# Two-PSUM-bank multiplies and transposed key sums in a strided-attention kernel

## The chip, the cores and the metric

The kernel runs on one core of one Trainium2 chip. The metric is device time in microseconds (us), the median of several executions. The time before is 129.94 us (three runs, 129.86 to 130.21). A profile covers one execution; its span is about 2 us shorter than the device time, because the span runs from the first instruction to the last. Fast runs are the undisturbed ones, slow runs the others.

Engines in the profile: PE (TensorE matmul), PEld (its weight loads), DVE (VectorE), ACT (ScalarE), POOL (GpSimd), SP (which issues the transfers). PSUM is the memory that the matmuls write into. In this kernel a one-bank PSUM tile holds 512 float32 values in each of the 128 partitions, a two-bank tile 1024. "Tail" below means the time from the end of VectorE's last multiply to the end of the span.

## The reference

```python
Q, K, V: (8, 12, 1024, 64) float32, stride 64
k = K[:, :, ::64]; v = V[:, :, ::64]              # 16 keys per head
scores = q @ k.T / 8
w = exp(scores - max); w = w / (sum(w) + 1e-10)
result = w @ v                                     # same shape as V
```

Each of the 96 heads has 1024 queries and only 16 keys. There is little arithmetic: 25 MB of queries come in, 25 MB of results go out.

## The kernel before

Four heads make a group, so there are 24 groups, and a group is one 1 MB load and one 1 MB store. GpSimd casts the queries to bf16, VectorE transposes them in 32x32 blocks, PE makes scores, ScalarE takes the exponential, PE makes key sums and outputs, and VectorE multiplies the outputs by the reciprocal sums. These are the parts that the change touches:

```python
psum_o = ... bufs=4        # one bank each;  OBUFS = 9 output tiles

def keys(m):               # m = 0 at the start, 1 and 2 after groups 2 and 4
    for h in range(4):
        nc.vector.tensor_scalar(out=k_m[...h], in0=kr, scalar1=slot_m[:, h:h+1], ..., op0=mult)
    for u in range(2):
        kp = psum_o.tile([P, 2, 2, 2, 4 * NK], FP32)     # one bank
        ... four matmuls into kp ...
        nc.scalar.copy(k_t half, kp)

def sums(g):
    sm = psum_s.tile([P, 2, 8, 2], FP32)
    for i in range(8):
        nc.tensor.matmul(sm[:, :, i], lhsT=wt[g][:, i], rhs=s_sel, ...)   # 4 columns
    nc.vector.reciprocal(rec[g], sm ...)

def outputs(g, c):         # c = 0..3
    ps = psum_o.tile([P, 2, 2, 2 * D], FP32)             # one bank
    for i in range(2):
        nc.tensor.matmul(ps[:, :, i], lhsT=wt[g][:, 2 * c + i], rhs=vb[g], ...)
    nc.vector.tensor_tensor(out=out_sb[g][...], in0=ps, in1=rec[g] broadcast, op=mult)   # 512

for g in range(NG):
    transpose(g + 2); sums(g); outputs(g, 0); outputs(g, 1); scores(g + 1)
    outputs(g, 2); outputs(g, 3); values(g + 2); cast(g + 3)
    if g in (2, 4): keys(g // 2)
    store(g); load(g + QBUFS)
# ... cut: set-up, scores, values, cast, load, store ...
```

The softmax here doesn't subtract the row's maximum and nothing guards it: scores larger than these inputs give would overflow.

Of the kernel before, what the change touches and what calls it, by code (L numbers as in the profile page):

```python
# [11 lines left out]
FP32 = mybir.dt.float32  # L12
BF16 = mybir.dt.bfloat16
# [6 lines left out]
def _ap_with(ap: bass.AP, new_ap, extra_offset: int = 0) -> bass.AP:  # L20
    return dataclasses.replace(
        ap, ap=[list(p) for p in new_ap], offset=ap.offset + extra_offset
    )
# [22 lines left out]



@with_exitstack
def kernel(  # L50
    ctx: ExitStack,
# [7 lines left out]
    nc = tc.nc  # L59

    B, H, S, D = Q.shape
    NK = S // stride
    scale = 1.0 / math.sqrt(D)

    P = 128
# [4 lines left out]
    KW = P + NK  # L70
    assert B * H == NG * HG and S == 1024 and D == 64 and NK == 16
    QBUFS = 10
    OBUFS = 9

    const = ctx.enter_context(tc.tile_pool(name="const", bufs=1))
    qn_pool = ctx.enter_context(tc.tile_pool(name="qn", bufs=QBUFS))
    out_pool = ctx.enter_context(tc.tile_pool(name="outsb", bufs=OBUFS))
    qb_pool = ctx.enter_context(tc.tile_pool(name="qb", bufs=2))
    qt_pool = ctx.enter_context(tc.tile_pool(name="qt", bufs=2))
    vb_pool = ctx.enter_context(tc.tile_pool(name="vb", bufs=3))  # L80
    rec_pool = ctx.enter_context(tc.tile_pool(name="rec", bufs=2))
    psum_sc = ctx.enter_context(tc.tile_pool(name="psc", bufs=2, space=bass.MemoryType.PSUM))
    psum_o = ctx.enter_context(tc.tile_pool(name="po", bufs=4, space=bass.MemoryType.PSUM))
    psum_s = ctx.enter_context(tc.tile_pool(name="psm", bufs=2, space=bass.MemoryType.PSUM))

    ctx.enter_context(tc.manual_schedule())
# [7 lines left out]
    def load(g):  # L94
        qn[g] = qn_pool.tile([P, 32 * D], FP32, name="qn", tag="qn")
        n = P if g < 2 else 32
        _copy(nc, qn[g], _ap_with(Q, [[HG * SD // n, n], [1, HG * SD // n]], g * HG * SD))
# [12 lines left out]
    perm_k = const.tile([P, 2, 2, 2, NK], BF16, name="perm_k")  # L110
# [10 lines left out]
    for c in range(2):  # L121
        for a in range(2):
            for e in range(2):
                nc.gpsimd.tensor_copy(
                    out=perm_v[:, c, a, :, e], in_=id_v[:, c, :, a]
                )

    k_t = const.tile([P, NG, 2, KW], BF16, name="k_t")
    nc.vector.memset(k_t[:, 0:8], 0.0)  # L129
    w_bufs = []  # L130
    for i in range(3):
# [7 lines left out]
        out=slot_i, in0=iota_p, scalar1=4, scalar2=3,  # L139
# [4 lines left out]
    s_sel = const.tile([P, 4], BF16, name="s_sel")  # L144
    nc.vector.tensor_scalar(  # L145
        out=s_sel, in0=col4, scalar1=slot_f, scalar2=None, op0=ALU.is_equal
    )
    slot_m = const.tile([P, 4], FP32, name="slot_m")
    nc.vector.tensor_copy(out=slot_m, in_=s_sel)
    mask = const.tile([P, 4, D], BF16, name="mask")  # L150
# [2 lines left out]
    k_m = const.tile([P, NC, 2, 4, 32], BF16, name="k_m")  # L153
# [4 lines left out]
    def keys(m):  # L158
        kr = k_raw[:, 4 * m : 4 * m + 4].rearrange("p n (q f) -> p n f q", f=2)
        for h in range(4):  # L160
            nc.vector.tensor_scalar(  # L161
                out=k_m[:, 4 * m : 4 * m + 4, :, h], in0=kr,
                scalar1=slot_m[:, h : h + 1], scalar2=None, op0=ALU.mult,
            )
        for u in range(2):
            kp = psum_o.tile([P, 2, 2, 2, 4 * NK], FP32, name="kp", tag="o")
            for i in range(2):
                for f in range(2):
                    nc.tensor.matmul(  # L169
                        kp[:, i, :, f],  # L170
                        lhsT=k_m[:, 4 * m + 2 * u + i, f].rearrange("p h q -> p (h q)"),
                        rhs=perm_k.rearrange("p c a b k -> p c (a b k)"),
                        start=True, stop=True,
                    )
            g0 = 8 * m + 4 * u
            dst = k_t[:, g0 : g0 + 4]
            nc.scalar.copy(  # L177
                _ap_with(dst, [dst.ap[0], [KW, 8], [32, 4], [1, NK]], extra_offset=NK),
                kp.rearrange("p i c f (s k) -> p (i c f) s k", s=4),
            )  # L180


    def value_rows():
# [10 lines left out]
    qb, qt, wt, vb, rec, out_sb = {}, {}, {}, {}, {}, {}  # L194


    def values(g):
        vb[g] = vb_pool.tile([P, 4, D], BF16, name="vb", tag="vb")
        nc.gpsimd.tensor_tensor(  # L199
            out=vb[g], in0=mask,  # L200
            in1=v_rep[:, g // 2, g % 2].unsqueeze(1).to_broadcast([P, 4, D]),
            op=ALU.mult,
        )

    def cast(g):
        qb[g] = qb_pool.tile([P, 32 * D], BF16, name="qb", tag="qb")
        nc.gpsimd.tensor_copy(out=qb[g], in_=qn[g])  # L207

    def transpose(g):
        qt[g] = qt_pool.tile([P, 32 * D], BF16, name="qt", tag="qt")  # L210
        nc.vector.transpose(qt[g].bitcast(I32), qb[g].bitcast(I32))  # L211

    def scores(g):
        sc = psum_sc.tile([P, 512], FP32, name="sc", tag="sc")
        q = qt[g]
        for e in range(2):
            for f in range(2):
                nc.tensor.matmul(  # L218
                    sc, lhsT=k_t[:, g, f, NK * (1 - e) : NK * (1 - e) + P],
                    rhs=_ap_with(  # L220
                        q, [q.ap[0], [2 * D, 8], [16 * D, 2], [2, 32]],
                        extra_offset=D * e + f,
                    ),
                    start=e + f == 0, stop=e + f == 2,
                )
        w = wt[g] = w_bufs[g % 3]
        for a in range(2):
            wa = w[64 * a : 64 * a + 64]
            nc.scalar.activation(  # L229
                out=_ap_with(wa, [wa.ap[0], [P, 8], [1, 2], [2, 32]], extra_offset=64 * a),  # L230
                in_=sc[64 * a : 64 * a + 64].rearrange("p (t x q) -> p t x q", t=8, x=2),
                func=AF.Exp, bias=0.0, scale=scale,
            )

    def sums(g):
        sm = psum_s.tile([P, 2, 8, 2], FP32, name="sm", tag="sm")
        for i in range(8):
            nc.tensor.matmul(  # L238
                sm[:, :, i], lhsT=wt[g][:, i], rhs=s_sel, start=True, stop=True
            )  # L240
        rec[g] = rec_pool.tile([P, 2, 16], FP32, name="rec", tag="rec")
        nc.vector.reciprocal(rec[g], sm.rearrange("p b i e -> p b (i e)"))  # L242

    def outputs(g, c):
        if c == 0:
            out_sb[g] = out_pool.tile([P, 2, 16, D], FP32, name="out_sb", tag="out_sb")
        ps = psum_o.tile([P, 2, 2, 2 * D], FP32, name="o_ps", tag="o")
        for i in range(2):
            nc.tensor.matmul(  # L249
                ps[:, :, i], lhsT=wt[g][:, 2 * c + i],  # L250
                rhs=vb[g].rearrange("p s d -> p (s d)"),
                start=True, stop=True,
            )
        nc.vector.tensor_tensor(  # L254
            out=out_sb[g][:, :, 4 * c : 4 * c + 4],
            in0=ps.rearrange("p b i (e d) -> p b (i e) d", e=2),
            in1=rec[g][:, :, 4 * c : 4 * c + 4].unsqueeze(3).to_broadcast([P, 2, 4, D]),
            op=ALU.mult,
        )

    def store(g):
        o = out_sb[g]
        _copy(
            nc,
            _ap_with(out, [[16 * D, P], [2 * SD, 2], [1, 16 * D]], g * HG * SD),
            _ap_with(o, [o.ap[0], [1, 1], [1, 32 * D]]),
        )

    keys(0)
    cast(0)  # L270
    transpose(0)
    scores(0)
    value_rows()
    values(0)
# [4 lines left out]
    for g in range(NG):  # L279
        if g + 2 < NG:  # L280
            transpose(g + 2)
        sums(g)
        outputs(g, 0)
        outputs(g, 1)
        if g + 1 < NG:
            scores(g + 1)
        outputs(g, 2)
        outputs(g, 3)
        if g + 2 < NG:
            values(g + 2)  # L290
        if g + 3 < NG:
            cast(g + 3)
        if g in (2, 4):
            keys(g // 2)
        store(g)
        if g + QBUFS < NG:
            load(g + QBUFS)
# [35 lines left out]
```

## Time and profile before

| before | value | where it is read |
|---|---|---|
| span | 127.7 us | page, first line |
| DMA queue, share of 16 engines | 96.8%, 51.12 MB | page, part 3 |
| VectorE busy | 109.2 us, 85% | page, part 1 |
| VectorE's cycle per group | 3.97 us | timeline of VectorE |
| end of the last multiply | 119.97 us | timeline of VectorE |
| from there to the end of the span | 7.7 us | difference |

The page says that two resources are nearly full. These are its parts 1, 3 and 4 (engines, the DMA queue with its share, and the chain of work that ended last), and two groups of its part 5, whose columns are busy us and mean ns of one, then idle time in front and its releaser:

```profile
PE 73.3 (57%) x508; PEld 38.6 (30%) x508; DVE 109.2 (85%) x170; ACT 39.6 (31%) x55; POOL 66.7 (52%) x69
...
q1 hardware_dynamic: 7904, 51.12, 96.8%
...
DVE 2%; DVEq 0%; issue 0%
...
L254 DVE TENSOR_TENSOR out_sb<-o_ps,rec 128x512 f32<-128x512 f32 x96 | 59.9, 685 | 4.8 <-PE o_ps L249 2.6
...
L242 DVE RECIPROCAL rec<-sm 128x32 f32<-128x32 f32 x24 | 7.8, 326 | 0.3 <-PE sm L238 0.3
```

The chain covers only 2% of the span: it is followed from the last multiply back to 117.14 us and breaks off there. Such a short chain is no proof of a limit (the run with the large memset below shows the same 2%, with VectorE late). The sign of a DMA limit is the queue, which is nearly full to the end. But VectorE is hardly slower. This is its timeline of the kernel before (start, duration, instruction):

```profile
62.61 1.24 DVE L211 STREAM_TRANSPOSE qt<-qb 128x1024 int32<-128x1024 int32 x1
63.77 0.32 DVE L242 RECIPROCAL rec<-sm 128x32 f32<-128x32 f32 x1
64.18 2.48 DVE L254 TENSOR_TENSOR out_sb<-o_ps,rec 128x512 f32<-128x512 f32 x4
66.58 1.24 DVE L211 STREAM_TRANSPOSE qt<-qb 128x1024 int32<-128x1024 int32 x1
```

From one query transpose to the next is 3.97 us with no gap. Read the distances between starts, not the durations: independent instructions overlap by about 0.08 us, and an instruction that needs the result of the last starts a little after its end (here 0.09 us: the reciprocal ends at 64.09, the first multiply starts at 64.18).

### The profile page before, as it was taken

The numbers are of one execution on the slowest core, as the hardware profiler recorded it, in microseconds if no ns is written. First come the engines' busy times: TensorE is split into PE (matmuls) and PEld (weight loads), VectorE is DVE, ScalarE is ACT, GpSimd is POOL, SyncE is SP. The second block draws the span as 40 slices with busy tenths as digits, with TensorE's granted clock in tenths as the row PEclk, the third lists the DMA queues.
The fourth block names the chain that finished last, engine by engine and source line by source line (L and its number), as shares of the span: only waits on it lengthen the run. The fifth ranks groups of instructions, "written<-read, shape, count | busy, mean of one in ns | idle before, by whom it ended". The sixth has DMA issues, their size and how long they took to land. (4 is left out here: it accounts for less than half of the span.)

```text
span 127.7 us, 1518 instructions
## 1 busy us (share of the span) xinstructions
PE 73.3 (57%) x508; PEld 38.6 (30%) x508; DVE 109.2 (85%) x170; ACT 39.6 (31%) x55; POOL 66.7 (52%) x69
## 2 busy tenths in 40 slices
PE   0006767974476097866675579755567776674000
PEld 0003233441433063333342234432234323342000
DVE  6997468999979987899999999999999999999500
ACT  3003404224244134344424440444431344323000
POOL 8980499675217605387767635787555727000000
PEclk9999999999779855599999965799998559999555
DMA  2999989898998998989989999999999999999981
GB/s 70 380 322 459 482 339 482 349 482 359 462 472 336 503 400 377 505 346 431 493 344 439 454 385 436 441 408 452 426 398 464 385 421 431 426 416 428 421 372 46
DMA packets 7913, 51.23 MB, mean 401 GB/s; under 512 B 3872, under 2 KB 3872, under 8 KB 3872
## 3 DMA queue, kind: packets, MB, share of 16 engines
q1 hardware_dynamic: 7904, 51.12, 96.8%
q8 instruction: 4, 0.07, 0.2%
q14 instruction: 5, 0.04, 0.1%
HBM read 25.95 MB, written 25.17 MB: 400 GB/s over the span
## 5 line engine op out<-in xcount | busy, mean ns | idle before, releaser
L254 DVE TENSOR_TENSOR out_sb<-o_ps,rec 128x512 f32<-128x512 f32 x96 | 59.9, 685 | 4.8 <-PE o_ps L249 2.6
L229 ACT ACTIVATE w<-sc 64x512 bf16<-64x512 f32 x48 | 35.1, 732 | 60.0 <-PE sc L218 56.7
L207 POOL CAST qb<-qn 128x2048 bf16<-128x2048 f32 x24 | 45.5, 1898 | 0.4 <-DMA qn<-in_Q_dram 0.4
L249 PE MATMUL o_ps<-vb,w 128*128 128x256 bf16 x192 | 38.0, 321 | 2.4 <-DVE out_sb L254 1.4
L199 POOL TENSOR_TENSOR vb<-mask,v_rep 128x256 bf16<-128x256 bf16 x24 | 16.1, 670 | 40.3 <-PE o_ps L249 35.4
L218 PE MATMUL sc<-qt,k_t 128*128 128x512 bf16 x96 | 32.7, 472 | 1.5 <-DVE qt L211 1.2
L211 DVE STREAM_TRANSPOSE qt<-qb 128x1024 int32<-128x1024 int32 x24 | 29.7, 1237 | 1.6 <-POOL qb L207 1.6
L249 PEld LDWEIGHTS <-w 128*128 128x128 bf16 x192 | 19.3, 110 | 16.2 <-issue 8.6
L238 PE MATMUL sm<-s_sel,w 128*128 128x4 bf16 x192 | 8.7, 167 | 22.1 <-ACT w L229 22.1
L238 PEld LDWEIGHTS <-w 128*128 128x128 bf16 x192 | 6.9, 100 | 30.1 <-ACT w L229 29.6
L218 PEld LDWEIGHTS <-k_t 128*128 128x128 bf16 x96 | 10.8, 114 | 12.0 <-issue 6.5
L169 PE MATMUL kp<-perm_k,k_m 128*128 128x128 bf16 x24 | 3.1, 311 | 17.5 <-DVE k_m L161 17.5
L242 DVE RECIPROCAL rec<-sm 128x32 f32<-128x32 f32 x24 | 7.8, 326 | 0.3 <-PE sm L238 0.3
L169 PEld LDWEIGHTS <-k_m 128*128 128x128 bf16 x24 | 2.3, 141 | 18.2 <-DVE k_m L161 18.2
L177 ACT CAST k_t<-kp 128x512 bf16<-128x512 f32 x6 | 3.2, 590 | 14.1 <-PE kp L169 14.1
L161 DVE TENSOR_SCALAR k_m<-k_raw,slot_m 128x256 bf16<-128x256 f32 x12 | 6.8, 626 | 0.0
L192 DVE CAST v_rep<-vp 128x384 bf16<-128x384 f32 x4 | 2.2, 558 | 2.6 <-PE vp L188 2.6
L135 POOL MEMSET k_t<- 128x4608 bf16 x1 | 3.9, 3938 | 0.0
L145 DVE TENSOR_SCALAR s_sel<-col,slot_f 128x4 bf16<-128x4 int16 x1 | 3.2, 3155 | 0.1
L188 PE MATMUL vp<-v_bf,perm_v 128*128 128x384 bf16 x4 | 2.0, 489 | 0.8 <-DVE v_rep L192 0.6
L177 ACT ACT_TABLE_LOAD x1 | 1.3, 1283 | 2.1 <-DVE k_t L129 2.1
L129 DVE MEMSET k_t<- 128x1152 uint32 x1 | 1.0, 1018 | 1.0 <-PEq L314 1.0
(17 smaller groups left out, 6.3 us busy)
## 6 DMA issues: line engine op xcount, KB each, us to landing
qn<-in_Q_dram SPq DMA_DIRECT2D x24, 1024.0 KB, 13.9
out_dram<-out_sb SPq DMA_DIRECT2D x24, 1024.0 KB, 12.0
k_raw<-in_K_dram SPq DMA_DIRECT2D x1, 384.0 KB, 4.1
v_raw<-in_V_dram SPq DMA_DIRECT2D x1, 384.0 KB, 7.2
```

Source lines behind the costliest of these rows:

```text
L161: nc.vector.tensor_scalar(out=k_m[:, 4 * m : 4 * m + 4, :, h], in0=kr, scalar1=slot_m[:, h : h + 1], scalar2=None, op0=ALU.mult,)
L169: nc.tensor.matmul(kp[:, i, :, f], lhsT=k_m[:, 4 * m + 2 * u + i, f].rearrange("p h q -> p (h q)"), rhs=perm_k.rearrange("p c a b k -> p c ...
L177: nc.scalar.copy(_ap_with(dst, [dst.ap[0], [KW, 8], [32, 4], [1, NK]], extra_offset=NK), kp.rearrange("p i c f (s k) -> p (i c f) s k", s=4),)
L199: nc.gpsimd.tensor_tensor(out=vb[g], in0=mask, in1=v_rep[:, g // 2, g % 2].unsqueeze(1).to_broadcast([P, 4, D]), op=ALU.mult,)
L207: nc.gpsimd.tensor_copy(out=qb[g], in_=qn[g])
L211: nc.vector.transpose(qt[g].bitcast(I32), qb[g].bitcast(I32))
L218: nc.tensor.matmul(sc, lhsT=k_t[:, g, f, NK * (1 - e) : NK * (1 - e) + P], rhs=_ap_with(q, [q.ap[0], [2 * D, 8], [16 * D, 2], [2, 32]], ex ...
L229: nc.scalar.activation(out=_ap_with(wa, [wa.ap[0], [P, 8], [1, 2], [2, 32]], extra_offset=64 * a), in_=sc[64 * a : 64 * a + 64].rearrange( ...
L238: nc.tensor.matmul(sm[:, :, i], lhsT=wt[g][:, i], rhs=s_sel, start=True, stop=True)
L242: nc.vector.reciprocal(rec[g], sm.rearrange("p b i e -> p b (i e)"))
L249: nc.tensor.matmul(ps[:, :, i], lhsT=wt[g][:, 2 * c + i], rhs=vb[g].rearrange("p s d -> p (s d)"), start=True, stop=True,)
L254: nc.vector.tensor_tensor(out=out_sb[g][:, :, 4 * c : 4 * c + 4], in0=ps.rearrange("p b i (e d) -> p b (i e) d", e=2), in1=rec[g][:, :, 4 ...
```

## The change

The intent is fewer and larger instructions. A VectorE multiply covers two PSUM banks (1024 elements, two per group in place of four). The key sums come from four matmuls, each with a 32-column selector as weights on its own 32 columns of the array, in place of eight 4-column ones. They now lie along the free dimension, and VectorE turns them with a 32x32 transpose before the reciprocal. Matmul and weight-load instructions per group fall from 40 to 32.

```diff
-    OBUFS = 9
+    OBUFS = 8
-    psum_o ... bufs=4
+    psum_o ... bufs=2                        # two banks each
 def keys(m):
-        for u in range(2):  one-bank kp, four matmuls, nc.scalar.copy
+        kp = psum_o.tile([P, 4, 2, 2, 4 * NK], FP32)   # two banks
+        ... eight matmuls, then one nc.scalar.copy of 1024 elements
 def sums(g):
-        sm = psum_s.tile([P, 2, 8, 2], FP32)
-        for i in range(8):
-            nc.tensor.matmul(sm[:, :, i], lhsT=wt[g][:, i], rhs=s_sel, ...)
-        nc.vector.reciprocal(rec[g], sm ...)
+        sm = psum_s.tile([P, 8, 32], FP32)
+        for q in range(4):
+            nc.tensor.matmul(sm[32*q : 32*q+32], lhsT=sel32,
+                             rhs=wt[g][:, :, 32*q : 32*q+32], ..., tile_position=(0, 32*q))
+        nc.vector.transpose(smt, sm)
+        nc.vector.reciprocal(rec[g], smt[:, :, 0:4])
 def outputs(g, c):                           # c = 0, 1
-        ps = psum_o.tile([P, 2, 2, 2 * D], FP32);  two matmuls, multiply of 512
+        ps = psum_o.tile([P, 4, 4, D], FP32);      four matmuls, multiply of 1024
# cut: sel32 made at set-up, query order in scores, order of calls in the loop
```

## The prediction

> **What bounds it now.** (a) DMA: the page's queue table has the dynamic queue at 96.8% of 16 engines' span, 51.12 MB; my fine windows show about 420 GB/s from 4 us until 123.5 us. (b) VectorE. Its timeline is a closed chain from 20.65 us (first reciprocal) to 119.98 us (last multiply), repeating every 3.98 us per group: transpose of Q (start to next start 1.16), reciprocal (0.42 to the first multiply), four 512-element multiplies (0.60 apart, 2.40). The only gaps are about 2.9 us between 34 and 54 us, waiting for PE around the key groups. Replaying the issues at 420 GB/s, the last store (issued at 120.0) finds only about 0.6 MB ahead of it: DMA keeps pace with VectorE at the end, with 1 to 1.5 us of slack. So VectorE faster gains little (DMA floor); VectorE slower shows almost fully.
>
> **Removed.** Per group: two of four multiplies' fixed costs, eight key-sum matmuls (0.35 us of PE), the reciprocal's PSUM source. PE is not on the chain in most groups: VectorE's waits for it total 5.5 us, 2.6 of these in start-up.
>
> **Added.** A 128x256 fp32 transpose on VectorE, PSUM to SBUF, and a second dependent step (transpose, reciprocal, multiply). The Trainium skill, "VectorE: DVE Perf Modes", section "The perf-mode tier table", caps a tensor_tensor with a PSUM operand at one element per cycle; the trace agrees (512 elements, 600 ns apart, 533 of it at 0.96 GHz). So a two-bank multiply is no faster per element:
> - multiply of 1024: 1067 + 67 = 1.13 us apart; two = 2.27. Saves 0.13 a group.
> - new transpose: the Q transpose takes 1237 ns for 1024 elements, 170 over one per cycle; so 256 take about 0.43, plus 0.04 to 0.11 that the trace shows between dependent ops: +0.50.
> - reciprocal, 32 elements from SBUF: about 0.30 (was 0.33), same wait after it.
>
> Group: 1.16 + 0.50 + 0.41 + 2.27 = 4.34 us against 3.98: +0.36, times 24 = +8.6 us, all on the chain.
>
> **Moved.** Start-up: one 1024-element key copy on ScalarE (about 1.05 us, after eight matmuls) replaces two of 0.53; scores of group 0 used to start after the first. That delays the first scores and all behind them by about 1 us. Key-group stalls on PE stay near 3 us (key product now takes one of two output buffers). OBUFS 8: at most five stores are outstanding now (longest landing 17.8 us over 3.98), so no effect. The tail shortens by about 1 us, the store queue being nearly empty.
>
> **Sum.** 129.9 + 8.6 + 1.0 - 1.0 = 138.5; I shade it to 137.5 for a cheaper reciprocal and some regained PE stalls. Range 133 to 141. Slower by over 2%: 0.91; within: 0.07; faster: 0.02.
>
> **What shows each step.** VectorE group cycle about 4.3 us in the timeline; multiply near 1.22 us each, 48 of them; new transpose near 0.43; first reciprocal about 1 us later; last multiply ends near 128 to 130 us; DMA share about 90%, dips below 0.9 in the last third; PE busy falls without effect.
>
> **What would make it wrong.** The transpose out of PSUM or the SBUF reciprocal far cheaper than estimated (below 0.3 and 0.2 would give 133); PE stalls vanishing; or the column-tiled matmuls draining PE so that sums arrive late (the sums have about 2 us of slack), which would exceed 141. If the time stays at 130, my view that VectorE and DMA finish together is wrong.

## The result and the profile after

The changed kernel takes 134.04 us (four runs, 133.46 to 134.25). Its ratio to the kernel before is 1.0315, 95% interval 1.0267 to 1.0364. A ratio here is over fast runs alone, so it is not quite the ratio of the medians quoted.

These are the same parts of the page for the changed kernel:

```profile
PE 77.7 (59%) x412; PEld 38.5 (29%) x412; DVE 114.8 (87%) x148; ACT 39.4 (30%) x52; POOL 66.6 (50%) x69
...
q1 hardware_dynamic: 7904, 51.12, 93.4%
...
DVE 78%; PE 9%; issue 3%; POOL 3%; DVEq 1%; ACT 1%; POOLq 0%
...
L262 DVE TENSOR_TENSOR out_sb<-o_ps,rec 128x1024 f32<-128x1024 f32 x48 | 56.7, 1220 | 4.8 <-PE o_ps L257 2.5
...
L246 DVE STREAM_TRANSPOSE smt<-sm 128x256 f32<-128x256 f32 x24 | 9.9, 411 | 0.3 <-PE sm L240 0.3
L250 DVE RECIPROCAL rec<-smt 128x32 f32<-128x32 f32 x24 | 8.5, 353 | 0.8
```

The chain can now be followed through VectorE for 78% of the span. Since a chain can also break off, that alone proves little; the transfers, below, show that the limit has changed. VectorE's timeline of the changed kernel shows what was added:

```profile
64.63 1.23 DVE L213 STREAM_TRANSPOSE qt<-qb 128x1024 int32<-128x1024 int32 x1
65.79 0.41 DVE L246 STREAM_TRANSPOSE smt<-sm 128x256 f32<-128x256 f32 x1
66.23 0.35 DVE L250 RECIPROCAL rec<-smt 128x32 f32<-128x32 f32 x1
66.67 2.36 DVE L262 TENSOR_TENSOR out_sb<-o_ps,rec 128x1024 f32<-128x1024 f32 x2
68.95 1.23 DVE L213 STREAM_TRANSPOSE qt<-qb 128x1024 int32<-128x1024 int32 x1
```

The cycle is 4.32 us. The two multiplies take 2.28 from start to the next start (before: 2.40), which saves 0.12. The transpose of the sums and the gap of 0.03 behind it put in 0.44, the reciprocal and its gap 0.44 where 0.41 stood.

The transfers are no longer always busy. These are two stretches of the changed kernel and then, as third line, the later stretch of the kernel before. The columns are start and end, length, busy us (and number of instructions) of PE, PEld, DVE, ACT and POOL, granted TensorE clock, busy share of the DMA engines and GB/s:

```profile
90.00:105.00 15.00, 10.41 (x60) 5.23 (x58) 14.62 (x18) 5.27 (x8) 8.03 (x8) 0.89 1.01 426
105.00:120.00 15.00, 9.56 (x55) 4.75 (x53) 14.50 (x19) 4.95 (x7) 5.18 (x5) 0.89 0.80 330
105.00:120.00 15.00, 8.24 (x76) 4.79 (x76) 14.61 (x25) 4.50 (x7) 2.64 (x3) 0.96 1.01 422
```

From 105 to 120 us the changed kernel moves 330 GB/s where the kernel before moved 422. In this stretch of the changed kernel the loads are over, and each VectorE cycle makes only one 1 MB store available.

The books of the two profiles:

| term | before | after | difference |
|---|---|---|---|
| VectorE's closed chain starts (third query transpose) | 19.48 us | 20.39 us | +0.9 |
| 24 cycles | 3.97 us each | 4.32 us each | +8.3 |
| the two later key scalings, four instructions each | 2.19 + 1.84 us | 1.13 + 1.13 us | -1.8 |
| VectorE's waits for PE on the chain after that start | 2.9 us | 2.85 us | -0.05 |
| last multiply ends (the sum of the four is +7.4) | 119.97 us | 127.18 us | +7.2 |
| from there to the end of the span | 7.73 us | 5.22 us | -2.5 |
| span | 127.7 us | 132.4 us | +4.7 |

VectorE finishes 7.2 us later and the kernel only 4.7 us. The prediction had a number for the cycle and the start; the third and the sixth rows are its misses, and the experiments take them up. Each column is one execution. The same changed kernel, profiled again as a yardstick below, divided the third and fourth rows otherwise (2.51 us of scalings, 2.44 of waits) and ended its last multiply within 0.02 us of the first profile.

### The profile page after: what moved, and what is told of

Read it like the earlier page. It is cut to its first block, busy times and chain, and to the rows that moved or that the text cites. A ratio compares the mean times of both kernels' runs of the same rounds, so it can differ in the third digit from the quotient of the medians.

```text
span 132.4 us, 1301 instructions
## 1 busy us (share of the span) xinstructions
PE 77.7 (59%) x412; PEld 38.5 (29%) x412; DVE 114.8 (87%) x148; ACT 39.4 (30%) x52; POOL 66.6 (50%) x69
## 3 DMA queue, kind: packets, MB, share of 16 engines
q1 hardware_dynamic: 7904, 51.12, 93.4%
## 4 chain that ended last, share of the span: by engine, by line
DVE 78%; PE 9%; issue 3%; POOL 3%; DVEq 1%; ACT 1%; POOLq 0%
DVE out_sb L262 40%; DVE qt L213 17%; DVE rec L250 6%; DVE smt L246 6%; PE sc L220 4%; DVE k_m L165 4%; PE o_ps L257 3%; DVE s_sel L146 2%; PE kp L172 2%; POOL qb L209 2%; DVE w L134 1%; POOL vb L201 1%; DVEq L334 1%; ACT k_t L179 1%; DVE k_t L130 1%
## 5 line engine op out<-in xcount | busy, mean ns | idle before, releaser
L262 DVE TENSOR_TENSOR out_sb<-o_ps,rec 128x1024 f32<-128x1024 f32 x48 | 56.7, 1220 | 4.8 <-PE o_ps L257 2.5
L257 PE MATMUL o_ps<-vb,w 128*128 128x256 bf16 x192 | 35.1, 314 | 10.2 <-DVE out_sb L262 10.1
L257 PEld LDWEIGHTS <-w 128*128 128x128 bf16 x192 | 19.2, 110 | 26.1 <-DVE out_sb L262 13.1
L240 PE MATMUL sm<-w,sel 128*32 128x256 bf16 x96 | 14.3, 312 | 15.1 <-ACT w L231 14.9
L240 PEld LDWEIGHTS <-sel 128*32 128x32 bf16 x96 | 6.3, 95 | 26.5 <-issue 26.4
L246 DVE STREAM_TRANSPOSE smt<-sm 128x256 f32<-128x256 f32 x24 | 9.9, 411 | 0.3 <-PE sm L240 0.3
L250 DVE RECIPROCAL rec<-smt 128x32 f32<-128x32 f32 x24 | 8.5, 353 | 0.8
L179 ACT CAST k_t<-kp 128x1024 bf16<-128x1024 f32 x3 | 3.0, 1012 | 15.8 <-PE kp L172 15.8
L165 DVE TENSOR_SCALAR k_m<-k_raw,slot_m 128x256 bf16<-128x256 f32 x12 | 5.0, 480 | 0.0
```

Source lines behind the costliest of these rows:

```text
L165: nc.vector.tensor_scalar(out=k_m[:, 4 * m : 4 * m + 4, :, h], in0=kr, scalar1=slot_m[:, h : h + 1], scalar2=None, op0=ALU.mult,)
L240: nc.tensor.matmul(sm[32 * q : 32 * q + 32], lhsT=sel32, rhs=wt[g][:, :, 32 * q : 32 * q + 32], start=True, stop=True, tile_position=(0, 3 ...
L246: nc.vector.transpose(smt.rearrange("p i r -> p (i r)"), sm.rearrange("p i r -> p (i r)"))
L250: nc.vector.reciprocal(rec[g], smt[:, :, 0:4])
L257: nc.tensor.matmul(ps[:, i].rearrange("p s d -> p (s d)"), lhsT=wt[g][:, 4 * c + i], rhs=vb[g].rearrange("p s d -> p (s d)"), start=True, ...
L262: nc.vector.tensor_tensor(out=out_sb[g][:, :, 4 * c : 4 * c + 4].rearrange("p s i d -> p i s d"), in0=ps, in1=rec[g][:, 4 * c : 4 * c + 4] ...
```

## The experiments

Theory A is mine: VectorE's chain got longer by the transpose and the step that hangs on it, the kernel before stood on the transfers with only a little slack under VectorE, and above that slack each microsecond of VectorE shows. Rival B says that two double-bank output buffers in place of four single ones stall PE and VectorE. The other question is where 2.5 us of VectorE's delay went.

### Direct sums, two-bank multiplies

```diff
 changed kernel, sums(g):
-        four column-tiled matmuls; nc.vector.transpose(smt, sm); reciprocal(rec, smt[:, :, 0:4])
+        sm = psum_s.tile([P, 8, 4], FP32)
+        for i in range(8):
+            nc.tensor.matmul(sm[:, i], lhsT=wt[g][:, i], rhs=s_sel, ...)
+        nc.vector.reciprocal(rec[g], sm)
```

> The changed kernel with the key sums done directly again (eight 4-column matmuls, reciprocal straight from PSUM, no 32x32 transpose); the two-bank multiplies stay. Theory A (the transpose and the step that hangs on it put about 0.46 us per group on VectorE's chain, and the two-bank multiply takes off 0.13): VectorE's group cycle falls from 4.32 to about 3.86 us, below the 3.98 of before; the last multiply ends near 116 us; but the transfers (51 MB at about 420 GB/s) then end the kernel, so the time is 129.5 us, 128.7 to 130.3, no better than before by more than 1%. Rival B (the loss comes from having two double-bank output buffers instead of four single ones): cycle stays over 4.2 us and the time at 133 to 134.5.

Measured: correct, 129.54 us, ratio to before 0.9984 (0.9964 to 1.0004). VectorE's cycle is 3.84 us, and the last multiply ends at 117.90 us, 2.1 us before that of the kernel before. The span is the same 127.7 us. These are stretches at the end of this run's profile (same columns as above):

```profile
112.00:118.00 6.00, 2.65 (x25) 1.47 (x22) 5.72 (x7) 1.46 (x2) 0.00 (x0) 1.00 1.01 419
118.00:124.00 6.00, 0.00 (x0) 0.00 (x0) 0.00 (x0) 0.00 (x0) 0.00 (x0) 0.57 1.00 422
```

After 118 us no compute engine works, and the transfers still run at full rate for six more microseconds. Rival B falls: the two double-bank buffers are in this kernel too (as are the new query order and the new layout of the output tile), and it runs the shortest cycle so far. The two-bank multiply alone makes VectorE faster and the kernel no faster.

### Transposed sums, one-bank multiplies

```diff
 changed kernel:
+    psum_o with four one-bank buffers, key product copied in two halves, as before
 outputs(g, c), c = 0..3:
+        ps = psum_o.tile([P, 2, 4, D], FP32);  two matmuls, multiply of 512
```

> The other half alone: column-tiled key sums and the transpose, with four one-bank multiplies, four one-bank output buffers and the two-step key copy of before. Theory A: group cycle 3.98 + 0.47 = 4.45 us, last multiply ends near 130.5 us, time 136 to 138 us, slower than the changed kernel. Rival B: the four buffers bring it back to 130 or 131.

Measured: correct, 135.77 us, ratio 1.0470 (1.0445 to 1.0494). The cycle is 4.45 us, as expected. The last multiply ends at 128.47 us and not at 130.5, so the time lies just under the expected range; the key scalings took 1.13 and 1.20 us here, a saving that the expectation had not counted. So the two halves of the change have opposite signs. Against 3.97 us the transposed sums cost 0.48 us per cycle and the two-bank multiply saves 0.13, and together they give 4.32.

### Key product copied in halves, first try

```diff
 changed kernel, keys(m):
-        eight matmuls into kp; one copy
+        for u in range(2): four matmuls into half u of kp; copy of that half
```

> The changed kernel, but the key product is copied in two halves, the first after four of the eight matmuls. Theory A: the first score matmul starts 0.9 us earlier (11.6 instead of 12.5 us), the chain with it, group cycle unchanged at 4.32, and as VectorE alone sets the end the whole 0.9 us shows: 133.1 us where the changed kernel has 134.0. If start-up is hidden elsewhere: no difference from the changed kernel.

Measured: correct, 135.75 us, ratio 1.0474 (1.0444 to 1.0504), worse than the changed kernel. The first scores started at 12.03 us, only 0.48 earlier than the 12.51 of the changed kernel. The timeline of this run at the first later key step shows what the edit had brought in (the brackets give idle time and what ended it):

```profile
34.13 0.61 PE L173 MATMUL kp<-perm_k,k_m 128*128 128x128 bf16 x4 [4.35 <-DVE k_m L165]
34.83 0.58 ACT L180 CAST k_t<-kp 128x512 bf16<-128x512 f32 x1 [3.90 <-PE kp L173]
35.47 0.59 PE L173 MATMUL kp<-perm_k,k_m 128*128 128x128 bf16 x4 [0.73 <-ACT k_t L180]
...
36.44 0.45 DVE L247 STREAM_TRANSPOSE smt<-sm 128x256 f32<-128x256 f32 x1 [1.22 <-PE sm L241]
```

The second four matmuls write the other half of the same tile, and they were made to wait for the copy of the first half. That wait went to VectorE at both later key steps (1.22 and 0.95 us). The experiment tested my edit, not the question. Two separate tiles are needed; that run follows below.

### Direct sums and this split together

> Direct sums, two-bank multiplies and the split key copy together: the version that should be best. Theory A: VectorE's last multiply ends near 115 us, but transfers set the end: 128.8 to 130 us, within 0.4 us of the run with direct sums alone. If VectorE still set the end it would gain 0.9 us on that run.

The edit is the sum of the first and the third. Measured: correct, ratio 1.0027 (0.9983 to 1.0071). One of the six executions (132.73 us) was slow; the median of the five fast ones is 129.67 us (130.25 with the slow one). It carries the same new wait (2.1 us of VectorE waiting for sums), and VectorE ended at 120.76 us and not at 115. It says nothing about the best version and is replaced below. Its profile is of a slower execution (130.82 us; three others took 129.65 to 129.67): the span was 129.1 us although VectorE ended only 0.8 us later than in the kernel before, so the end that the transfers set also moves by more than 1 us between executions. Why was not found.

### VectorE delay alone, in the kernel before: small and large

```diff
 kernel before (with OBUFS = 8, to make room):
         outputs(g, 3)
+        nc.vector.memset(junk[:, 0:16], 0.0)     # second kernel: 0:300
```

> The kernel before with one useless 16-element VectorE memset per group after the last multiply (about 0.11 us each, 2.6 us in all; eight output tiles instead of nine, for room). Theory A: in the changed kernel the last store lands 5.3 us after the last multiply, in the kernel before 7.7 us, as its store waits behind earlier ones; so the first 2.4 us that VectorE loses are absorbed there: time within 0.6 us of before (130 to 130.6). If every microsecond of VectorE counts: 132.5.

> The same with a 300-element memset (about 0.34 us each, 8 us in all: what the changed kernel's cycle adds). Theory A: 8.1 - 2.4 = 5.7 us slower than before, 134.7 to 136.5, the last multiply ending near 128 us and the tail near 5.3 us: a pure VectorE delay without any other part of the change makes the same loss. If the changed kernel's loss came from PE or PSUM buffers, there is no reason for this one to match it; a DMA-bound kernel would stay near 130.

A memset fills a tile with a constant; here it only takes VectorE's time. Measured, small: correct, 129.95 us, ratio 1.0012 (0.9998 to 1.0025). It gave hardly any dose: the cycle went from 3.97 to 3.98 us, since this 0.07 us memset runs beside the start of the next transpose. The key steps took less than in the kernel before, so VectorE even ended earlier, at 118.47 us, and the kernel was no faster. It did not test the slack. It does show that eight output tiles in place of nine cost nothing that the interval can show.

Measured, large: correct, 131.9 us, ratio 1.0163 (1.0116 to 1.0211), and not 134.7. The verdict at a 2% mark is "unclear", but the interval lies above 1. The six executions fall into two groups (130.85 to 131.21 and 132.58 to 132.63), and the profile is of the first. The cycle rose by 0.27 us and not 0.34, and the key scalings fell from 4.03 to 2.24 us together. VectorE therefore ended at 124.11 us, 4.1 us later than before and not 8. The tail after it was 5.29 us, as in the changed kernel, and the transfers dip in the same stretch:

```profile
105.00:120.00 15.00, 10.55 (x77) 5.33 (x75) 14.60 (x27) 5.83 (x8) 3.17 (x3) 0.79 0.89 371
```

So the size was missed and the mechanism held: VectorE 4.1 us later, less 2.4 us taken up in the tail, makes 1.7 us of span (127.7 to 129.4; the medians differ by 2.0). A pure VectorE delay, with nothing else of the change, moves the kernel off the transfers in the same way.

Every run in which VectorE ended after 124 us has a tail of 5.2 to 5.3 us. The kernel before has 7.73 us, the direct sums 9.80 us. Subtracting, the kernel before had 2.5 us of slack under VectorE. This is a difference of two tails; no run put a dose smaller than the slack on VectorE and showed it vanish.

### Key product in halves, from two tiles

The changed kernel itself ran beside the next two as a yardstick.

> The changed kernel itself, as the yardstick on this chip for the two runs beside it: 133.5 to 134.5 us, 1.03 times before, VectorE's last multiply ending near 127.2 us.

Measured: correct, 134.07 us, ratio 1.0321 (1.0300 to 1.0342), last multiply at 127.17 us.

```diff
 changed kernel, keys(m):
+        if m == 0:
+            for u in range(2):
+                kh = psum_sc.tile([P, 2, 2, 2, 4 * NK], FP32)   # one bank, score pool
+                four matmuls into kh; nc.scalar.copy(k_t half u, kh)
+            return
```

> The changed kernel with the first key product in two separate one-bank tiles (borrowed from the score pool), each copied after its own four matmuls; the later key products as in the changed kernel. The earlier split run failed because its second four matmuls waited for the copy of the first half of the same tile. Theory A: first scores at 11.6 us instead of 12.5, first key-sum transpose 0.9 us earlier, time 0.9 us (0.5 to 1.3) below the changed kernel run beside it. If start-up is hidden: same time.

Measured: correct, 133.34 us, 0.73 us below the yardstick by medians; the ratios to before are 1.0285 (1.0260 to 1.0310) and 1.0321. The first scores start at 11.70 us and not at 12.51, and the third query transpose at 19.58 and not at 20.39. So the start-up term is real, 0.8 us on VectorE's chain, and 0.5 (from the ratios) to 0.7 us (from the medians) of it shows in the time. The two intervals overlap, so the size of that gain is uncertain. The profile is of the fastest of the five executions (132.73 us): VectorE ended 1.5 us before the yardstick there, since the key steps also took less.

### A GpSimd cast beside the later key scalings

In the kernel before, a GpSimd cast was under way at both later key scalings. These are GpSimd's and VectorE's timelines of that kernel:

```profile
30.81 1.89 POOL L207 CAST qb<-qn 128x2048 bf16<-128x2048 f32 x1
...
31.44 2.19 DVE L161 TENSOR_SCALAR k_m<-k_raw,slot_m 128x256 bf16<-128x256 f32 x4
...
41.69 1.89 POOL L207 CAST qb<-qn 128x2048 bf16<-128x2048 f32 x1
...
42.67 1.84 DVE L161 TENSOR_SCALAR k_m<-k_raw,slot_m 128x256 bf16<-128x256 f32 x4
```

In the changed kernel the casts were over or ending (at 32.60 and 45.01), and four scalings took 1.13 us:

```profile
33.39 1.13 DVE L165 TENSOR_SCALAR k_m<-k_raw,slot_m 128x256 bf16<-128x256 f32 x4
...
44.98 1.13 DVE L165 TENSOR_SCALAR k_m<-k_raw,slot_m 128x256 bf16<-128x256 f32 x4
```

The Trainium skill, "SBUF — State Buffer", section "Who interferes with whom", says that a `tensor_scalar` in a two-port mode and a GpSimd instruction lock each other out for a whole instruction. Whether these scalings ran in such a mode, the trace does not say. This run tests the lock-out here:

```diff
 changed kernel, in the loop:
         if g in (2, 4):
+            nc.gpsimd.tensor_copy(out=junk, in_=out_sb[g] ...)   # 2048 elements, useless
             keys(g // 2)
```

> The changed kernel plus one useless GpSimd cast of 2048 elements at each of the two later key steps, released by the same multiply that releases VectorE's key scaling. In the kernel before a GpSimd cast was under way at both key scalings (2.19 and 1.84 us for four), in the changed one at neither (1.13 us). If the scaling waits while such a cast runs: the scalings take 2.5 to 3 us each, the last multiply ends 2.5 to 4 us later, time 136.5 to 138. If the two do not interfere: scalings 1.13 us, time as the changed kernel beside it.

Measured: correct, 142.29 us, ratio 1.0955 (1.0935 to 1.0976). The direction was right and the size was missed: 8.2 us and not 2.5 to 4. The timelines of this run:

```profile
33.39 4.80 DVE L165 TENSOR_SCALAR k_m<-k_raw,slot_m 128x256 bf16<-128x256 f32 x4
33.54 1.95 POOL L302 CAST junk<-out_sb 128x2048 bf16<-128x2048 f32 x1 [3.62 <-DVE out_sb L264]
35.45 0.70 POOL L203 TENSOR_TENSOR vb<-mask,v_rep 128x256 bf16<-128x256 bf16 x1
36.10 1.95 POOL L211 CAST qb<-qn 128x2048 bf16<-128x2048 f32 x1
38.12 1.23 DVE L215 STREAM_TRANSPOSE qt<-qb 128x1024 int32<-128x1024 int32 x1
```

The useless cast held back the two GpSimd instructions behind it, and the scalings lasted as long as all three. Taken one by one, the first scaling took 0.34 us and the other three 1.98, 0.75 and 1.97 us: each ended 0.14 to 0.15 us after one of the GpSimd instructions. The second key step repeats this (4.82 us). So the scalings do pay for GpSimd work that runs at the same moment.

The other traces settle the 1.8 us that the changed kernel won there. In all runs together there are ten later key steps whose first scaling a cast delayed, and in each this scaling ended 0.14 to 0.15 us after the cast; where nothing of GpSimd was in its way, one scaling took 0.33 to 0.35 us (once 0.23, behind a memset). In the kernel before the two delayed ones took 1.41 and 1.05 us, 1.8 us more than two free ones. That the casts of the changed kernel no longer coincide because its cycle has shifted against them is likely, not tested; in the yardstick run one of them did coincide, for 0.25 us.

The run with the useless cast also confirms the slope: VectorE ended at 135.31 us, 8.1 us later than the yardstick, and the time rose by 8.2.

### The best version, and the transfers alone

```diff
 best version: changed kernel + direct sums + first key product from two tiles
 transfers only: kernel before without any compute; store(g) stores a tile of zeros
```

> The version the experiments point to: two-bank multiplies, direct key sums, and the first key product copied in halves from two separate tiles. VectorE's last multiply should end near 115 to 117 us, 3 to 5 us before that of the kernel before. Theory A (transfers set the end once VectorE ends before about 119): 129.2 to 129.9 us, no more than 0.6% below before. If VectorE still set the end: 126 to 127.

> Wrong result on purpose (all zeros are stored): the same loads and stores in the same order, all compute taken out, each store ready as soon as the queue reaches it. It measures how low the transfers alone can get. Theory A (before and the direct-sums version lie on the transfer floor): span 124.5 to 127.5 us, time 126.5 to 129.5 us, DMA share 96% or more throughout. If the floor is much lower, below 123 us, then the direct-sums version is held by something else than transfers, and my account of why it gained nothing is wrong.

Measured, best version: correct, 129.63 us, ratio 0.9976 (0.9964 to 0.9989). VectorE ends at 116.70 us, 3.3 us before that of the kernel before, and the span is again 127.7 us. It is 0.24% faster than the kernel before, and the only correct version whose interval lies below 1.

Measured, transfers only (wrong result): 127.41 us, ratio 0.9837 (0.9806 to 0.9868), span 126.4 us. This is its DMA row of the page (busy tenths in 40 slices) and its queue line:

```profile
DMA  2999999997989999999989989899899999999992
...
q1 hardware_dynamic: 7904, 51.12, 97.4%
```

With all compute gone, the kernel before would lose 2.5 us. That is about the most that any change to the compute engines could have won while the transfers stay as they are. This profile, too, is of a slower execution (128.20 us); four of the six had a span of 125.6 us. Why the best version stops 1.3 to 2.1 us of span above this, although VectorE ends early, was not tested.

## Why the prediction was right, and where its terms were off

- **The limits, and the direction: right.** The kernel before stood on the transfers with VectorE close under them. The direct-sums run and the transfers-only run show the floor, the large memset shows that VectorE's delay alone breaks through it.
- **The cost per group: right.** Predicted 4.34 us, measured 4.32: multiplies 1.13 us apart (1.14), transpose 0.43 us long (0.41), reciprocal 0.30 (0.35). The cap that the prediction took from the Trainium skill, "VectorE: DVE Perf Modes", section "The perf-mode tier table", holds: 1024 elements took 1220 ns and 512 took 685, so 512 more elements cost 535 ns, 1.04 ns each, and doubling the size saved only the fixed part. The same page's section "Rules for kernel authors" says to minimize the number of operations; that is true here, and worth 0.12 to 0.13 us for two multiplies, against 0.44 for the transpose with its gap.
- **The start: right.** About 1 us predicted, 0.9 read, 0.8 of the chain recovered by copying the first key product in halves from two tiles, with 0.5 to 0.7 us of time.
- **"DMA keeps pace with VectorE at the end, with 1 to 1.5 us of slack", and the tail "shortens by about 1 us": mis-sized.** The slack was 2.5 us (7.73 against 5.22 us from last multiply to end). I had estimated the data queued ahead of the last store, but I had no lone store to measure the tail with; the changed kernel and six further runs give it as 5.2 to 5.3 us.
- **Missed: the key scalings.** The sum had no term for GpSimd locking VectorE out, which gave back 1.8 us. The duration was in the trace before: one instruction form that took 339 ns at the least and 1.41 us where a cast ran.
- The unshaded sum was 138.5 us. With the tail 1.5 us shorter and the scalings 1.8 us shorter it comes to 135.2, and the measured time is 134.04. The spans differ by 4.7 us and the medians by 4.1, and the cycle's term was 0.3 us too large; that covers most of the rest. The shading to 137.5 was made for a cheaper reciprocal (it was not cheaper) and for fewer PE stalls (they stayed at 2.9 us), so it pointed the right way for the wrong reasons.
- **The number: low in the range, and partly luck.** The forecast slowdown was 7.6 us and the measured one 4.1. The range reached down to 133 for a far cheaper transpose or reciprocal, which did not come; the two terms that did fail were not on the prediction's list of what could make it wrong. VectorE's last multiply ended at 127.18 us, just below the "128 to 130", and the DMA share was 93.4%, not "about 90%".
- **"PE busy falls": wrong, without effect.** It rose from 73.3 to 77.7 us at the same mean clock (0.858 and 0.857). In its profile VectorE waited 0.3 us in all for the new sums.

## What to carry to other kernels

When two resources finish nearly together, cost a change on both: a gain on the one below the limit buys next to nothing, and a loss first uses up the slack and then counts in full. Measure that slack as the time from the last instruction to the end, against the same time in a run where the engine is plainly late. Fewer and larger instructions save only the fixed part of each (here about 0.06 us per multiply), so one added dependent instruction on the same engine can cost more than they save.

## What the Trainium skill lacked or had wrong

- "SBUF — State Buffer", section "Who interferes with whom": it says that the instruction issued first keeps the shared ports for its whole length. The runs agree. It does not say how the ports pass on when both engines have several instructions ready: beside three GpSimd instructions of 1.95, 0.70 and 1.95 us one scaling got through for each, and these took 1.98, 0.75 and 1.97 us.
- "VectorE: DVE Perf Modes", section "The TRN2 errata — SBUF-src ops pay a fixed extra latency per instruction": its table gives PSUM sources a larger fixed cost than SBUF sources (120 against 58 cycles). The 32-element reciprocal took a mean of 326 ns from PSUM and 353 ns from SBUF here, and the first figure includes overlap with the transpose in front. In the last two groups of the kernel before no transpose stands in front, and there it took 0.35 us from PSUM too. The source patterns also differ, so only the lack of a gain is shown.
- "TensorEngine Tiling (Array Packing)", section "Performance Considerations": it advises against taking the tiling factor from a dimension that is already small, but shows no measured case of trading many narrow matmuls for a few wide tiled ones. Here four column-tiled matmuls of 256 columns per group took 14.3 us of PE busy time over the 24 groups, and eight of 4 columns 8.7 us.
- None of the pages read shows what a memset costs when it is put between different VectorE instructions of a full chain: a 16-element one added 0.01 us per group, a 300-element one 0.27 us.
